# Conditioning units loaded into the accumulator a group ahead, in the first MLP of a two-layer diffusion backbone

## The chip, the cores and the metric

The kernel runs on one core of a Trainium2 chip. It uses five engines: TensorE (PE in the profile, its weight loads PEld), VectorE (DVE), ScalarE (ACT), GpSimd (POOL) and SyncE (SP), which here only issues DMA transfers from one queue. The metric is the device time of one execution in microseconds (us); lower is better. Everything is computed in float32. A product of two float32 matrices is made of three products in TensorE's fp32r format: each operand is split into a high part (a cast) and a low part (the rest, a subtraction), and high x high, high x low and low x high are summed.

## The reference

Two layers over 512 latent tokens and 256 context tokens of 1024 channels. The change lies in the first layer's MLP and in the conditioning computed beside it:

```python
def ada_mods(cond, w, b):
    m = (jax.nn.silu(cond) @ w + b)[..., None, :]
    return jnp.split(m, N_MOD, axis=-1)          # shift, scale, gate, twice

def sq_relu_mlp(h, w_in, w_out):
    return jnp.square(jax.nn.relu(h @ w_in)) @ w_out

# layer 0: mixer, then for latents and for the context, each with its own conditioning vector
x = x + gt2 * rms_norm(sq_relu_mlp(modulate(rms_norm(x, g), sh2, sc2), w_in, w_out), g_post)
```

`w_in` is 1024 x 4096, `w_out` 4096 x 1024, and `w_ada` 1024 x 6144 for each of two layers. A modulation is a vector (two of them, one for the latents and one for the context) times `w_ada`: little arithmetic, but 48 MB of weights to read.

## The kernel before, in words

The first MLP of layer 0 (`mlp0`, line 1127) has two phases. In the first, the 4096 hidden channels are made in 16 groups of 256 for all 768 tokens. Groups 2 to 15 use a Strassen-like scheme: seven products of half-size blocks instead of eight (`Seven`, line 894), each a chain of 12 matmuls of 384 columns, 84 in a group. The right-hand blocks are sums of activations made once (`sums`, tiles `sums` and `rb`), the left-hand ones sums of a group's weights (`weights_sums`, line 858), which VectorE and ScalarE make for group g + 1 while TensorE works on group g. In the profile these are the matmuls `psin<-...`. A group's results are evicted into the accumulator tile `acc` (128 partitions x 6144 floats) or, in the last group, into two tiles of the pool `work`, are squared there and leave for the DRAM tile `hidden`. Before the accumulator is needed for the second phase only its first half (3072 columns, four blocks of 768 in turn) is in use.

The second phase multiplies the hidden blocks by `w_out` in three rounds of seven products (`prep` prepares the operands of one, line 1190; matmuls `pso<-...`, 36 of 512 columns for a product), and then four plain groups. `prep(1)` makes the difference `t3` of two row blocks of `w_out` in the first 2048 columns of the accumulator; `prep(2)` and `prep(3)` use the same blocks and `t3` again. The first two hidden blocks go to the second half of the accumulator (`hid_load`), three row blocks to raw tiles (`row_load`).

Beside the first phase runs the conditioning that is due later, of three kinds of load, all of 1 MB:

- a group's weights, `sums_load(g + 2)`, issued in group g, used by `weights_sums` in the next group's turn (`raw<-in_w_mlp_in`);
- a conditioning unit, `ada_load`, half of a 1024 x 512 piece of `w_ada` for both conditioning vectors, multiplied on TensorE by `ada_mm` (4 matmuls `psada<-raw,cond`) in turn 3 of the groups 3 to 10: eight units, called 0 to 7 here;
- a lone slab, `lone_load`, 1024 x 256 of `w_ada` for the latents' vector alone, which VectorE multiplies and folds (`ada_sum`: one scaling, seven multiply-adds of 128 x 256, a transpose, a reduction into `parts`). Twelve slabs in groups 2 to 13; four make a modulation, which `ada_fin` completes with 4 selection matmuls (`psada<-parts,sel`).

All three take their tile from the ring `rawp` (line 79), three tiles of 128 x 2048, in the order in which the scheduler places them. A load waits on SyncE until the tile's last reader is done, and everything behind it on SyncE's queue waits too, because a queue issues in order. The order of every engine's instructions around the change is chosen at build time by a scheduler with its own model of times (`TC_OPTS`, line 40); the order in the program text is its input and sets which buffer a load gets. Before the change, the hidden blocks' load stands at group 15 in the text, and the scheduler has moved it up to group 2, since its place in the accumulator is free.

`raw_load` gives all 1 MB loads the same source line (L154), and nearly all engine instructions are recorded by one helper (L68), so tiles and shapes tell them apart in the profile.

Of the kernel before, what the change touches and what calls it, by code (L numbers as in the profile page):

```python
# [13 lines left out]
ALU = mybir.AluOpType  # L14
# [3 lines left out]
P = 128  # L18
D = 1024
# [34 lines left out]
def backbone(ctx: ExitStack, tc, x, c, ctx_in, c_ctx, w_ada, b_ada, g_mix_pre, g_mix_post,  # L54
# [104 lines left out]
    def work_tile():  # L159
        return tmp.tile([P, D], F32, tag="t", name="work")  # L160
# [130 lines left out]

    def ada_load(i, m, c0, width, u):
        nk = 2048 // width
        loaded[i, m, c0, u] = raw_load(w_ada[i, u * nk * P:(u + 1) * nk * P, m * D + c0:m * D + c0 + width]
                                       .rearrange("(k p) n -> p k n", p=P), width,
                                       rawp if (m, c0) == (SH2, 0) else None).rearrange("p (k n) -> p k n", n=width)
# [597 lines left out]
    class Seven:  # L894
# [11 lines left out]
        def run(self, between=None, turns={}):  # L906
# [4 lines left out]
            else:  # L911
                px, py = (psA.tile([P, 2, 512], F32, tag="a", name="psin") for _ in range(2))
                a, b, c, e = px[:, 0, 0:HN], px[:, 1, 0:HN], py[:, 0, 0:HN], py[:, 1, 0:HN]
            if g == NG - 1:
                r0, r1 = (work_tile()[:, 0:TOK] for _ in range(2))
            else:
                r0, r1 = (acc[:, TOK * z:TOK * z + TOK] for z in (2 * (g % 2), 2 * (g % 2) + 1))
            if g == 3:
# [208 lines left out]
    def mlp0(inner, order, extra, mid, last, before_last):  # L1127
# [62 lines left out]
        def prep(n):  # L1190
# [3 lines left out]
            end = c_ == NC - 1  # L1194
            t0 = X["t"] if "t" in X else acc[:, 0:2048]
            if z == 0:
                x, w = a(0, 0), b(0, 0)
            elif z == 1:
                x = done[c_, "s3"] = op(a(0, 0), a(0, 0), a(1, 0), ALU.subtract)
                w = done[c_, "t3"] = op(t0, b(1, 1), b(0, 1), ALU.subtract)  # L1200
            elif z == 2:
                x = op(X[1], a(1, 0), a(1, 1), ALU.add)
                w = op(b(0, 1), b(0, 1), b(0, 0), ALU.subtract)
            elif z == 3:
                x = op(X[0], a(1, 1), done[c_, "s3"], ALU.subtract)
                w = op(t0, done[c_, "t3"], b(0, 0), ALU.add)
            elif z == 4:
# [8 lines left out]
            wr = W[n % 3]  # L1216
            put(wr[:, 0:2048], wr[:, 2048:4096], w)
            xs[n] = [[q[:, k] for k in range(4)] for q in (hi, lo)]
# [11 lines left out]
            elif z == 6:  # L1230
                pair_load(4 * NC + 2, X[2]) if end else hid_load((c_ + 1, 1, 1), X[2])
                rows_load(4 * NC + 2) if end else row_load((c_ + 1, 1, 1))

        xs, ws = {}, {}
        for g in range(2, NG):
            now = products
            if g < NG - 1:
                products = weights_sums(g + 1)
            else:
                hid_load((0, 0, 0), acc[:, 3072:4608])  # L1240
                hid_load((0, 1, 0), acc[:, 4608:6144])
                for key in ((0, 0, 0), (0, 0, 1), (0, 1, 1)):
                    row_load(key)
            extra(g)
            seven = Seven(now, g)
            turns = {}
            if g == 2:
                turns[3] = lambda z: ada_end(*halves[1], z)
            elif g <= 10:
                half, u = halves[2 + (g - 3) // 2], (g - 3) % 2  # L1250
                ada_load(*half, 512, u)
                turns[3] = lambda z: ada_mm(*half, 512, u, z)
                if u:
                    turns[5] = lambda z: (ada_rows(*half), ada_end(*half, z))
            if g - 2 < 4 * len(lone):
                lone_load(g - 2)
            if g + 2 < NG:
                sums_load(g + 2)
            seven.run(lambda: mid(g), turns)
# [264 lines left out]
    def mid0(g):  # L1524
        n, j = divmod(g - 2, 4)
        if 0 <= n < len(lone):
            at = 32 * n + 8 * j
            ada_sum(*lone[n], j, 1, parts[0][:, at:at + 8], lone_raw.pop(g - 2))

# [5 lines left out]
    def extra0(g):  # L1535
# [4 lines left out]
        if g in (7, 8):  # L1540
            gate_away(0, GT2, g - 7)
        n, j = divmod(g - 6, 4)
        if j == 0 and 0 <= n < len(lone):
# [456 lines left out]
```

## Time and profile before

| | |
|---|---|
| Median of three runs | 1155.32 us (1154.81 to 1162.1) |
| Profiled execution | 1159.74 us, its span 1158.0 us |
| TensorE busy | 1125.4 us (97% of the span) |
| VectorE / ScalarE busy | 883.0 us (76%) / 668.7 us (58%) |
| Read from memory, written to it | 156.33 MB, 22.04 MB |
| First phase, groups 2 to 15 | about 122 to 358 us of the span |

The profile comes from one execution. A row of the timeline gives start and length in us, the engine, the operation with the tile that it writes and those it reads, shapes and a count, and in brackets the idle time before it with the work that ended it. `SPq` rows are DMA issues; a transfer lands some us later. In a row of the view of windows stand the stretch, its length, the busy time and count of each engine, and at the end the granted clock of TensorE (1.00 is full), the share of time that the DMA engines were busy, and GB/s.

### The profile page before, as it was taken

What the parts mean: (1) busy time and instruction counts of PE and PEld (TensorE: products, weight loads), DVE (VectorE), ACT (ScalarE), POOL (GpSimd) and SP (SyncE); (2) the same over time, 40 slices, a digit from 0 to 9 for tenths busy, and PEclk for the clock granted to TensorE, in tenths of its full rate; (3) what the DMA queues carried; (4) which work ended last, traced back from release to release, by engine and by line L of the source; (5) the groups of instructions that cost most, each with busy time, mean ns of one, the idle gap of its engine ahead of it and who ended that gap; (6) DMA issues with size and microseconds to landing.
All of it is one profiled execution on the core that took longest, in us unless ns stands there. A gap on an engine that the chain in (4) does not pass through costs nothing. (4 is left out here: it accounts for less than half of the span.)

```text
span 1158.0 us, 15507 instructions
## 1 busy us (share of the span) xinstructions
PE 1125.4 (97%) x6012; PEld 958.9 (83%) x6012; DVE 883.0 (76%) x1262; ACT 668.7 (58%) x1139; POOL 75.1 (6%) x82
## 2 busy tenths in 40 slices
PE   6999899999999999999999999999999999999998
PEld 5578788989988888888888889988988888888886
DVE  5799468777778887867478688977787779778875
ACT  6477345444456677765586468873775436445534
POOL 3040000000000000000231212100000000000000
PEclk9999999999999999999999999999999999999999
DMA  9996776676544443438141400046234124224304
GB/s 353 399 360 226 197 234 231 225 246 211 175 177 168 155 135 120 150 105 296 52 153 58 142 2 19 2 128 221 107 139 152 67 80 146 62 84 146 109 13 152
DMA packets 108490, 179.37 MB, mean 155 GB/s; under 512 B 7888, under 2 KB 67072, under 8 KB 108416
## 3 DMA queue, kind: packets, MB, share of 16 engines
q1 hardware_dynamic: 103712, 165.77, 42.6%
q10 hardware_dynamic: 4704, 12.61, 2.8%
q8 instruction: 47, 0.77, 0.3%
q14 instruction: 27, 0.22, 0.1%
HBM read 156.33 MB, written 22.04 MB: 154 GB/s over the span
## 5 line engine op out<-in xcount | busy, mean ns | idle before, releaser
L68 PE MATMUL pso<-rb,ra 128*128 128x512 f32 x576 | 134.9, 390 | 2.0 <-ACT m L68 1.2
L68 PEld LDWEIGHTS pso<-rb,ra 128*128 128x128 f32 x576 | 107.9, 188 | 25.5 <-ACT m L68 1.6
L68 PE MATMUL psin<-ra,rb 128*128 128x512 f32 (+2 forms) x468 | 117.5, 356 | 0.7 <-DVE acc L68 0.6
L68 DVE TENSOR_TENSOR acc<-acc,pso 128x512 f32<-128x512 f32 x90 | 60.6, 682 | 58.2 <-PE pso L68 58.2
L68 PE MATMUL psin<-ra 128*128 128x512 f32 (+1 forms) x340 | 96.3, 376 | 0.6 <-ACT work L68 0.6
L68 PEld LDWEIGHTS psin<-ra,rb 128*128 128x128 f32 x468 | 81.4, 189 | 12.7 <-issue 1.0
L68 PE MATMUL psin<-ra,units 128*128 128x384 f32 x434 | 81.8, 337 | 1.3 <-ACT psin L68 0.4
L68 PE MATMUL pso<-units,pairs 128*128 128x512 f32 x336 | 82.3, 389 | 0.0
L68 ACT CAST rb<-raw 128x2048 fp32r<-128x2048 f32 (+2 forms) x35 | 47.5, 1357 | 59.9 <-PE pso L68 54.8
L68 PEld LDWEIGHTS psin<-ra,units 128*128 128x128 f32 x434 | 75.2, 188 | 6.0 <-issue 1.7
L68 ACT CAST units<-raw 128x1024 fp32r<-128x1024 f32 (+2 forms) x47 | 49.4, 1078 | 52.9 <-DMA raw<-in_w_mlp_in 38.7
L68 PEld LDWEIGHTS pso<-units,pairs 128*128 128x128 f32 x336 | 63.1, 188 | 13.1
L68 PE MATMUL psin<-rb 128*128 128x512 f32 (+2 forms) x242 | 73.8, 357 | 0.0
L68 PEld LDWEIGHTS psin<-ra 128*128 128x128 f32 x340 | 62.7, 188 | 11.0 <-ACT work L68 1.0
L68 PE MATMUL psin<-rb,ra 128*128 128x512 f32 (+1 forms) x226 | 71.1, 367 | 0.0
L68 DVE TENSOR_TENSOR rb<-raw,rb 128x2048 fp32r<-128x2048 f32 (+2 forms) x41 | 61.3, 1494 | 10.1 <-ACT rb L68 9.9
L68 PE MATMUL psin<-sums,units 128*128 128x384 f32 x336 | 65.3, 342 | 2.7 <-ACT acc L68 2.7
L68 PEld LDWEIGHTS psin<-sums,units 128*128 128x128 f32 x336 | 59.9, 192 | 4.1 <-ACT acc L68 3.0
L68 DVE TENSOR_TENSOR units<-raw,units 128x1024 fp32r<-128x1024 f32 (+2 forms) x45 | 58.0, 1303 | 2.6 <-ACT units L68 2.5
L68 PE MATMUL pso<-units,ra 128*128 128x512 f32 x252 | 59.4, 389 | 0.0
L68 DVE TENSOR_TENSOR work<-raw 128x512 f32<-128x512 f32 (+1 forms) x42 | 35.5, 864 | 30.2 <-DMA raw<-in_w_mlp_in 25.2
L68 DVE SCALAR_TENSOR_TENSOR rows<-raw,cond,rows 128x256 f32<-128x256 f32 x112 | 53.5, 482 | 2.4
(253 smaller groups left out, 2411.0 us busy)
## 6 DMA issues: line engine op xcount, KB each, us to landing
raw<-in_w_ada SPq DMA_DIRECT2D x48, 1024.0 KB, 7.4
raw<-in_w_mlp_in SPq DMA_DIRECT2D x32, 1024.0 KB, 5.5
raw<-in_w_mlp_out SPq DMA_DIRECT2D x32, 1024.0 KB, 5.1
x<-hidden SPq DMA_DIRECT2D x14, 768.0 KB, 4.3
hidden<-acc ACTq DMA_DIRECT2D x26, 384.0 KB, 2.8
raw<-in_w_qkv SPq DMA_DIRECT2D x6, 1024.0 KB, 8.4
spill<-xl SPq DMA_DIRECT2D x8, 512.0 KB, 7.3
xl<-spill SPq DMA_DIRECT2D x8, 512.0 KB, 8.5
```

Source lines behind the costliest of these rows:

```text
L68: z = made(*args, **kw)
```

## The change

Conditioning units of groups 3 to 10 no longer take a tile of the ring. They have one home, columns 3072 to 5120 of the accumulator, and each is issued in turn 3 of the group before its own, right after the matmuls on its predecessor. In the ring remain the weights and the slabs; the weights' load is now written ahead of the slab's. A slab is folded one group after its load's group (`g - 3` instead of `g - 2`), and each `ada_fin` comes a group later. The hidden blocks' load, whose place overlaps the units' home, is written at group 14 and stands, after scheduling, behind the last unit. In the last group the results go to the accumulator as in the others; the two work tiles that they had are used by `prep(1)` for `t3`, cut in two halves with their own splits.

```diff
-    def ada_load(i, m, c0, width, u):
+    def ada_load(i, m, c0, width, u, home=None):
         nk = 2048 // width
+        if home is not None:
+            raw = loaded[i, m, c0, u] = home.rearrange("p (k n) -> p k n", n=width)
+            sy.dma_start(raw, w_ada[i, u * nk * P:(u + 1) * nk * P, m * D + c0:m * D + c0 + width]
+                         .rearrange("(k p) n -> p k n", p=P))
+            return
...
-            if g == NG - 1:
-                r0, r1 = (work_tile()[:, 0:TOK] for _ in range(2))
-            else:
-                r0, r1 = (acc[:, TOK * z:TOK * z + TOK] for z in (2 * (g % 2), 2 * (g % 2) + 1))
+            r0, r1 = (acc[:, TOK * z:TOK * z + TOK] for z in (2 * (g % 2), 2 * (g % 2) + 1))
...
-            t0 = X["t"] if "t" in X else acc[:, 0:2048]
+            t0 = X.get("t")
...
-                w = done[c_, "t3"] = op(t0, b(1, 1), b(0, 1), ALU.subtract)
+                if c_ == 0:
+                    w = done[c_, "t3"] = [op(work_tile(), b(1, 1)[:, q], b(0, 1)[:, q], ALU.subtract)
+                                          for q in (slice(0, 1024), slice(1024, 2048))]
+                else:
+                    w = done[c_, "t3"] = op(t0, b(1, 1), b(0, 1), ALU.subtract)
...
-                w = op(t0, done[c_, "t3"], b(0, 0), ALU.add)
+                if c_ == 0:
+                    for q, t3 in zip((slice(0, 1024), slice(1024, 2048)), done[c_, "t3"]):
+                        op(t0[:, q], t3, b(0, 0)[:, q], ALU.add)
+                    w = t0
+                else:
+                    w = op(t0, done[c_, "t3"], b(0, 0), ALU.add)
...
-            put(wr[:, 0:2048], wr[:, 2048:4096], w)
+            for q, src in enumerate(w if isinstance(w, list) else [w]):
+                z_ = slice(1024 * q, 1024 * q + src.shape[-1])
+                put(wr[:, 0:2048][:, z_], wr[:, 2048:4096][:, z_], src)
...
+        def unit_load(n):
+            if n < 8:
+                ada_load(*halves[2 + n // 2], 512, n % 2, acc[:, 3072:5120])
...
-            else:
+            if g == NG - 2:
                 hid_load((0, 0, 0), acc[:, 3072:4608])
                 hid_load((0, 1, 0), acc[:, 4608:6144])
+            if g == NG - 1:
                 for key in ((0, 0, 0), (0, 0, 1), (0, 1, 1)):
                     row_load(key)
...
+            if g + 2 < NG:
+                sums_load(g + 2)
+            if g - 2 < 4 * len(lone):
+                lone_load(g - 2)
             if g == 2:
-                turns[3] = lambda z: ada_end(*halves[1], z)
+                turns[3] = lambda z: (ada_end(*halves[1], z), unit_load(0))
             elif g <= 10:
                 half, u = halves[2 + (g - 3) // 2], (g - 3) % 2
-                ada_load(*half, 512, u)
-                turns[3] = lambda z: ada_mm(*half, 512, u, z)
+                turns[3] = lambda z: (ada_mm(*half, 512, u, z), unit_load(g - 2))
                 if u:
                     turns[5] = lambda z: (ada_rows(*half), ada_end(*half, z))
-            if g - 2 < 4 * len(lone):
-                lone_load(g - 2)
-            if g + 2 < NG:
-                sums_load(g + 2)
...
-        n, j = divmod(g - 2, 4)
+        n, j = divmod(g - 3, 4)
...
-            ada_sum(*lone[n], j, 1, parts[0][:, at:at + 8], lone_raw.pop(g - 2))
+            ada_sum(*lone[n], j, 1, parts[0][:, at:at + 8], lone_raw.pop(g - 3))
...
-        n, j = divmod(g - 6, 4)
+        n, j = divmod(g - 7, 4)
```

What the scheduler makes of it is read at three places. First SyncE's queue in groups 2 to 4: `raw<-in_w_mlp_in` is a group's weights, `128x8x256` of `in_w_ada` a slab, `128x4x512` of it a unit, `grows<-gc` two gate columns on their way to DRAM. Before:

```order
L154 DMA raw<-in_w_ada 128x8x256
L154 DMA raw<-in_w_mlp_in 128x8x256
L1167 DMA acc<-hidden 128x4x384 x2
L154 DMA raw<-in_w_ada 128x4x512
L411 DMA grows<-gc 128x8x1 x2
L154 DMA raw<-in_w_ada 128x8x256
L154 DMA raw<-in_w_mlp_in 128x8x256
L154 DMA raw<-in_w_ada 128x4x512
```

The same place in the changed program:

```order
L154 DMA raw<-in_w_mlp_in 128x8x256
L154 DMA raw<-in_w_ada 128x8x256
L296 DMA acc<-in_w_ada 128x4x512
L154 DMA raw<-in_w_mlp_in 128x8x256
L416 DMA grows<-gc 128x8x1 x2
L154 DMA raw<-in_w_ada 128x8x256
L296 DMA acc<-in_w_ada 128x4x512
L154 DMA raw<-in_w_mlp_in 128x8x256
```

Weights come first, the unit goes to the accumulator ahead of the next weights and of the gate columns, and the hidden blocks have left this place.

Second, VectorE from the last additions of group 14 (`acc<-acc,psin` x2) on to the split of the second product's weights in the second phase (`rb<-acc,rb` before, `rb<-work,rb` in two halves now); `rows` and `parts` belong to a slab, `x_` and `t_` are operands of the second phase. Before:

```order
L68 TENSOR_TENSOR acc<-acc,psin 128x384 x2
L68 TENSOR_TENSOR ra<-acc,ra 128x4x384
L68 TENSOR_TENSOR acc<-raw 128x2048
L68 TENSOR_TENSOR work<-work,psin 128x384
L68 TENSOR_TENSOR raw<-raw 128x2048
L68 TENSOR_TENSOR t_3133<-acc,raw 128x2048
L68 TENSOR_TENSOR work<-work,psin 128x384
L68 TENSOR_TENSOR x_3131<-acc,x_3132 128x1536
L68 TENSOR_TENSOR x_3130<-x_3132,acc 128x1536
L68 TENSOR_TENSOR rb<-acc,rb 128x2048
```

In the changed program, from the last multiply-add of the last slab:

```order
L68 SCALAR_TENSOR_TENSOR rows<-raw,cond,rows 128x256
L68 STREAM_TRANSPOSE raw<-rows 128x256
L68 TENSOR_REDUCE parts<-raw 128x8
L68 TENSOR_TENSOR acc<-acc,psin 128x384 x2
L68 TENSOR_TENSOR mods_103<-psada,cols 128x8
L68 TENSOR_TENSOR work<-raw 128x1024 x2
L68 TENSOR_TENSOR t_3128<-work,raw 128x1024
L68 TENSOR_TENSOR rb<-work,rb 128x1024
L68 TENSOR_TENSOR raw<-raw 128x2048
L68 TENSOR_TENSOR t_3128<-work,raw 128x1024
L68 TENSOR_TENSOR x_3126<-acc,x_3127 128x1536
L68 TENSOR_TENSOR x_3125<-x_3127,acc 128x1536
```

The difference of row blocks, before ahead of the last group's additions, now stands behind them and behind the last slab and its modulation; the split's second half (`rb<-work,rb`) follows the last row shown. Between the additions of group 14 and the first row shown stand the rest of that slab and the split `ra<-acc,ra`.

Third, TensorE from the last chains of group 15 (`psin`) to the second product of the second phase, with buffer numbers: `pso_3140`, `3141`, `3149` are the three tiles of the first product before, `pso_3135`, `3136`, `3144` now. Before (ten matmuls of the first tile stand further up, ahead of the last chains of group 14):

```order
L68 MATMUL psin_3015<-rb_111,ra_110 128x384 x12
L68 MATMUL pso_3140<-units_844,ra_110 128x512 x2
L68 MATMUL pso_3141<-units_844,ra_110 128x512 x12
L68 MATMUL psin_3013<-ra_110 128x384 x12
L68 MATMUL pso_3149<-units_844,ra_110 128x512 x12
L68 MATMUL pso_3163<-rb_111,ra_110 128x512
L68 MATMUL pso_3177<-rb_111,ra_110 128x512
L68 MATMUL pso_3201<-rb_111,ra_110 128x512
L68 MATMUL pso_3215<-rb_111,ra_110 128x512
L68 MATMUL pso_3163<-rb_111,ra_110 128x512 x11
```

In the changed program:

```order
L68 MATMUL psin_3007<-rb_111,ra_110 128x384 x12
L68 MATMUL pso_3135<-units_844,ra_110 128x512 x7
L68 MATMUL psada_2998<-parts_1067,sel_101 32x8 x4
L68 MATMUL psin_3005<-ra_110 128x384 x12
L68 MATMUL pso_3135<-units_844,ra_110 128x512 x5
L68 MATMUL pso_3136<-units_844,ra_110 128x512 x12
L68 MATMUL pso_3144<-units_844,ra_110 128x512 x12
L68 MATMUL pso_3158<-rb_111,ra_110 128x512
L68 MATMUL pso_3172<-rb_111,ra_110 128x512
L68 MATMUL pso_3158<-rb_111,ra_110 128x512 x6
L68 MATMUL pso_3172<-rb_111,ra_110 128x512 x6
L68 MATMUL pso_3197<-rb_111,ra_110 128x512 x7
```

All 36 matmuls of the first product now stand behind the group's next-to-last chain, with the last selection among them, and the second product starts with the matmuls that need only the first half of its weights. One matmul of the third product (`pso_3211`) follows, and then the rest of `pso_3158`, which needs the second half.

## The prediction

> **What bounds the kernel now.** I read the head of the page first, then who made TensorE wait in the stretch that the change touches (126 to 365 us), then the timeline around each of those waits.
>
> ```profile
> span 1158.0 us, 15507 instructions
> PE 1125.4 (97%) x6012; PEld 958.9 (83%) x6012; DVE 883.0 (76%) x1262; ACT 668.7 (58%) x1139; POOL 75.1 (6%) x82
> PE psin L68 <- ACT acc L68: 3.7, 3, 2.7
> PE psada L68 <- DMA raw<-in_w_ada: 3.4, 1, 3.4
> PE psada L68 <- DVE parts L68: 2.0, 1, 2.0
> PE pso L68 <- ACT m L68: 1.2, 1, 1.2
> PE psin L68 <- DVE acc L68: 0.6, 1, 0.6
> PE pso L68 <- DVE rb L68: 0.5, 1, 0.5
> ```
>
> TensorE bounds the program: 97% of the span. No matmul is removed, so the change can win only what TensorE loses in this stretch. The waits (columns: total us, times, longest) come to 11.4 us in the six rows. What a wait does to the clock is added to them:
>
> ```profile
> 140.20:143.50 3.30, 2.91 (x7) 1.25 (x8) 0.00 (x0) 0.00 (x0) 0.00 (x0) 0.50 0.66 39
> 191.40:194.70 3.30, 3.30 (x12) 3.30 (x11) 3.30 (x7) 1.52 (x3) 0.00 (x0) 0.50 0.32 117
> 331.70:336.00 4.30, 4.30 (x32) 4.28 (x33) 3.61 (x3) 2.62 (x3) 0.00 (x0) 1.00 1.04 409
> 166.22 4.32 PE L68 MATMUL psin<-ra,units 128*128 128x384 f32 x24
> 190.67 6.00 PE L68 MATMUL psin<-sums,units 128*128 128x384 f32 x24 [2.73 <-ACT acc L68]
> ```
>
> The third figure from the end of a window row is the granted clock. It was 0.50 right after the two longest waits and stayed 1.00 after the 2.0 us wait. The last two rows give its price: the same 24 matmuls took 4.32 us at full clock and 6.00 us after the wait, so 1.68 us. I put the same 1.7 us on the other long wait. The 4.32 us also give the pace: (4.32 - 0.34) / 23 = 0.173 us for a matmul of 384 columns; a group of 84 such matmuls is some 14.5 us, about 15.5 with its conditioning matmuls.
>
> The Trainium skill, "TensorE: Matmul & The Clock Gate", Part 1, says that the clock halves after an idle window of about 3.4 us or more. By that rule the wait of 2.73 us would have cost no clock, and the gain below would be 1.7 us smaller. The trace does not agree: 2.73 us was enough here, and the measurement decides.
>
> **Part 1, units in the accumulator, a group ahead.** The first long wait is for a conditioning unit:
>
> ```profile
> 126.36 0.92 SPq L1167 DMA_DIRECT2D acc<-hidden  x2
> 127.61 0.37 SPq L154 DMA_DIRECT2D raw<-in_w_ada  x1
> 132.97 2.35 PE L68 MATMUL psin<-rb 128*128 128x384 f32 x12
> 140.59 1.92 PE L68 MATMUL psada<-raw,cond 128*32 128x512 f32 x4 [3.35 <-DMA raw<-in_w_ada]
> DMA to landing us min/median/max: 5.0/6.6/12.9
> ```
>
> Unit 0 was issued at 127.61, behind 1.5 MB of hidden blocks (126.36), and TensorE idled 3.35 us for it. The last row is for the weight, slab and unit loads (1 MB each) issued from 115 to 345 us. In the changed queue the unit stands third after the loads that were issued at 116 and 117 us, and the hidden blocks have gone to the end of the phase. Three loads in a row at the shortest time land at 117.3 + 3 x 5.0 = 132.3. TensorE asks two matmuls after the row at 132.97 is through, at about 135.5. So this wait goes with its clock loss: 3.35 + 1.7 = **5.05 us**. What covers the load is 3 us of margin; each further us of lateness costs one.
>
> The write of two gate columns with 4-byte pieces stays on the queue, now behind unit 0 and the next weights. The slab and the unit after it wait there for that write's data, but both have a group of time.
>
> The seven later units have one home. A load can start only when the matmuls on the unit before it are through. In the changed order 74 to 144 matmuls of 384 columns stand between uses (12.8 us and more), but for one pair, units 1 and 2: there only 38 stand between, 38 x 0.173 = 6.6 us and some 0.1 for the tiny ones. Nearest rows: 5.0 us at the shortest, 6.6 the median, 12.9 at most. So the wait is 0 to 6.2 us, with 1.7 for the clock from 2.7 on. I take 0: the load of 12.9 us had hidden blocks and 4-byte writes around it, and here the weight load stands behind the unit.
>
> **Part 2, weights first in a ring of three that is theirs and the slabs'.**
>
> ```profile
> 178.84 1.06 PE L68 MATMUL psada<-raw,cond 128*32 128x512 f32 x8
> 179.97 0.37 SPq L154 DMA_DIRECT2D raw<-in_w_mlp_in  x1
> 188.46 1.05 ACT L68 CAST units<-raw 128x1024 fp32r<-128x1024 f32 x1 [3.73 <-DMA raw<-in_w_mlp_in]
> 190.16 0.46 ACT L68 COPY acc<-psin 128x384 f32<-128x384 f32 x1
> ACT units L68 <- DMA raw<-in_w_mlp_in: 38.7, 10, 6.8
> ```
>
> This is the second long wait, read backwards. TensorE idled to 190.67 for an eviction by ScalarE (190.16). That engine had stood in its order behind the cast of group 7's weights until they landed at 188.46. They were issued at 179.97, right after TensorE finished the conditioning matmuls of 178.84: the weights had to take that unit's slot. With the units elsewhere, a weight load takes the slot of the slab or the weights of a group earlier, freed about 15 us before. It then lands near 175 to 178 us, 10 us ahead of its cast. So 2.73 + 1.68 = **4.41 us** go. The row of 38.7 us (ten times that ScalarE waited for weights) shrinks too, but TensorE stands in none of the others, so I count nothing for them.
>
> SyncE's queue is in order, so the price of the new arrangement is that each weight load stands behind a slab that waits for the weights before it to be used, and behind a unit that waits for TensorE. All three come free early in a group, and the weights are asked for a group later, so this is hidden by 15 us less one landing, 5.0 to 12.9 us.
>
> **Part 3, slabs a group later.**
>
> ```profile
> 326.03 3.60 DVE L68 SCALAR_TENSOR_TENSOR rows<-raw,cond,rows 128x256 f32<-128x256 f32 x7
> 329.67 0.45 DVE L68 STREAM_TRANSPOSE raw<-rows 128x256 f32<-128x256 f32 x1
> 331.14 0.41 DVE L68 TENSOR_REDUCE parts<-raw 128x8 f32<-128x256 f32 x1
> 331.61 0.25 PE L68 MATMUL psada<-parts,sel 128*32 128x8 f32 x8 [2.01 <-DVE parts L68]
> ```
>
> The selection matmuls of the last slabs stood too early in TensorE's order and idled it for **2.01 us**, with no clock loss. In the changed order the folding of the last slab stands on VectorE ahead of the last group's two additions, and the selection behind the matmuls of the product that the second addition reads. Nothing waits there. The slab's work on VectorE (the 3.60 us and the short steps quoted) moves by a group and adds nothing.
>
> **Part 4, the step to the second matmul.** Here a wait changes its cause.
>
> ```profile
> 344.00 1.76 DVE L68 TENSOR_TENSOR ra<-acc,ra 128x1536 fp32r<-128x1536 f32 x1 [2.62 <-ACT ra L68]
> 350.87 2.24 PE L68 MATMUL psin<-rb,ra 128*128 128x384 f32 x12
> 350.88 2.29 DVE L68 TENSOR_TENSOR acc<-raw 128x2048 f32<-128x2048 f32 x1 [5.12 <-DMA hidden<-acc]
> 358.43 1.75 DVE L68 TENSOR_TENSOR x<-acc,x 128x1536 f32<-128x1536 f32 x1
> 361.77 2.28 DVE L68 TENSOR_TENSOR rb<-acc,rb 128x2048 fp32r<-128x2048 f32 x1
> 364.10 11.20 PE L68 MATMUL pso<-rb,ra 128*128 128x512 f32 x48 [0.55 <-DVE rb L68]
> DMA to landing us min/median/max: 5.0/5.0/8.3
> L68 DVE TENSOR_TENSOR units<-raw,units 128x1024 fp32r<-128x1024 f32 x12 | 14.6, 1220 | 0.0
> ```
>
> Before, the first difference of weight blocks (350.88) waited for the accumulator to be written out, its split ended at 361.77 + 2.28, and TensorE lost 1.2 + 0.5 us. Call T the end of the product at 350.87, so 353.1 there. In the changed program that difference goes to two work tiles, but stands on VectorE behind the last slab, the last additions and the sum of the selection, and needs the third block of rows, whose slot the last slab holds. The split at 344.00 ended at T - 7.3; ten matmuls of the second phase (2.3 us) no longer stand between, so T - 5.0; the slab's last multiply-add, transpose and reduction behind it (3.60 / 7 + 0.45 + 0.41 = 1.4) make T - 3.6 for the issue. It lands 5.0 to 8.3 us later (the row of landings, for the loads of 320 to 372 us): T + 1.4 to T + 4.7. The selection, seven matmuls of the second phase after T, allows T + 2 at the earliest. So the difference starts at S = T + 2 to T + 4.7; I take T + 2.5, since 5.0 is the median landing too.
>
> From S, VectorE has, in this order, two half differences, a half sum, a half split, a whole difference, a half sum, two x operations and the other half split: six halves of 1.22 (the mean in the last row), 2.28 and 2 x 1.75, in all 13.1 us. Cutting one operation in two costs 2 x 1.22 - 2.28 = 0.16 us, three times; it is in this sum. TensorE has 36 matmuls of 512 columns (11.20 / 48 = 0.23 us each), 12 of 384 and 22 more of 512 before it needs the other half: 8.3 + 2.1 + 5.1 = 15.5 us after T. S + 13.1 = T + 15.6, so hardly a wait. Three VectorE operations further (2.28 + 2.28 + 1.75 = 6.3) against 22 matmuls (5.1) it is T + 21.9 against T + 20.6, about 1.3 us. Between the ends the wait is 0.8 to 3.5 us, and 1.7 for the clock at the top. Against 1.7 us before I take **0**, with -0.9 to +3.5 as bounds. That the last group's results lie in the accumulator costs nothing: the same evictions write another place, free since group 13's results went out.
>
> **Sum.** 5.05 + 4.41 + 2.01 + 0 = 11.5 us off the profiled execution's 1159.74 us: 1148.3. (The span is 1158.0; 1.7 us lie around it and stay.) That execution is 4.4 us above the median shown (1155.32, of 1154.81 to 1162.1), which is just what one of the two long waits costs. If the usual run lacks one of them, the median comes down by 7.1 to 1148.2; if the 4.4 us are of another kind, by 11.5 to 1143.8. The first has the better reason, since the waits are races between transfers; I lean a little to the other side: **1147 us**.
>
> **The rivals.**
>
> *One home is too few.* Unit 2 lands late after unit 1, in the 38 matmuls. For it: 6.6 us is the median landing and also all the time there is. Against: the unit is first in its queue then. At 9 us the wait is 2.4 us, at 12.9 us 6.2 + 1.7: 1149 to 1155. Chance 0.13. The Trainium skill ("Trainium Kernel Development and Optimization", Best Practices) asks for double buffers to overlap transfers with work, and by it this home speaks against the change; the trace of before cannot show it.
>
> *The weights stay late.* The queue is in order, so a slab that waits holds the weights behind it, and the second long wait returns somewhere: 4.4 us less gain, 1151. For it: 38.7 us of such waits now. Against: the slack of a whole group. Chance 0.12.
>
> *Slower: the step to the second matmul.* The last slab holds the third row block's slot. If that block lands 8.3 us after a slab that itself was folded a group's half late (7 us), S is T + 12, the waits there are 12 + 13.1 + 6.3 - 20.6 = 10.8 us and two clock losses, 14.2 us in all, against 1.7 before: it eats the 11.5 us. From S = T + 12 on it is slower: 1156 to 1168. Against: slabs landed well before use in the rows above. Chance 0.05, most of it under 1%.
>
> *More goes than I count.* The small waits (1.0 of the row of 3.7 beside its 2.7, the row of 0.6) and the step's 1.7 go too and the 4.4 us are not a wait: 1143 or below. Chance 0.2.
>
> *It does not do what it says.* The scheduler could place the unit loads late; the order shows them a group ahead. Chance 0.02.
>
> **How the numbers follow.** My case has 0.48. About 1% (11.6 us) is what a measurement of this kernel can tell from no change, so it divides at 1143.8 and 1166.9. Faster by over 1% is the case of more, 0.2; slower by over 1% is the far part of the slower rival and of unforeseen waits in a new order, 0.03; the rest, 0.77, lies within. The range runs from 1142 (most of the case of more) to 1154 (both late-load rivals); what is left out is the slow step and the far end of the gain.
>
> **What would show it.** In the changed profile: no clock of 0.50 near 140 or 191 us; units landing before their matmuls, with unit 2 the nearest; ScalarE's wait for weights well under 38.7 us; no wait for the slabs' sums; and at the step a wait of 0 to 3 us for VectorE. Wrong would be a TensorE wait of over 2.7 us on a unit, on weights, or on the first split of the second phase.

## The result and the profile after

| us | before | after |
|---|---|---|
| median, measured side by side | 1158.12 | 1142.01 |
| spread of the times | 1154.81 to 1162.1 | 1141.47 to 1142.33 |
| ratio of the times, 95% interval | | 0.9859, 0.982 to 0.9898 |
| profiled execution | 1159.74 | 1141.98 |
| its span | 1158.0 | 1140.2 |

The change is faster by 1.4%: 16.1 us by the medians and 17.8 us by the two profiled executions. The median before is higher than the 1155.32 us given ahead of the prediction because a fourth time, 1160.91 us, has come to those three. The forecast was 1147 us, with most of the chance on a change of less than 1%; the gain is larger than that, and the time lies on the lower edge of the range of 1142 to 1154 us. In all the runs below one execution was slow (1269.16 us at a granted clock of 0.831, in the kernel "the same order without the home"); it counts in that kernel's median and not in its ratio.

TensorE's line in the head of the page after:

```profile
PE 1118.7 (98%) x6012; PEld 957.0 (84%) x6012; DVE 882.4 (77%) x1265; ACT 669.9 (59%) x1140; POOL 75.1 (7%) x82
```

The same 6012 matmuls are busy 6.7 us less (1125.4 before), and TensorE is idle 11.1 us less (span less busy time: 32.6 before, 21.5 now). The first figure is more than the two half-clock periods cost; what else is in it comes out below. Who makes TensorE wait from 115 to 370 us, after (columns as before: total us, times, longest):

```profile
PE pso L68 <- DVE ra L68: 0.3, 1, 0.3
PE psin L68 <- DVE mods L68: 0.3, 1, 0.3
```

Before, the six longest rows had 11.4 us there; now 0.6 us are left, and the granted clock is 1.00 throughout that stretch. The waits that I had counted went, and so did those that I had not. The timeline of after at the place of the old second wait (SyncE's queue, TensorE, ScalarE):

```profile
166.34 0.37 SPq L296 DMA_DIRECT2D acc<-in_w_ada  x1
171.28 0.37 SPq L154 DMA_DIRECT2D raw<-in_w_mlp_in  x1
...
173.58 1.06 PE L68 MATMUL psada<-acc,cond 128*32 128x512 f32 x8
...
176.56 1.05 ACT L68 CAST units<-raw 128x1024 fp32r<-128x1024 f32 x1 [0.84 <-DMA raw<-in_w_mlp_in]
```

The page's row of the units' loads after (count, size, median us to landing), and then ScalarE's waits for weights from 126 to 345 us:

```profile
acc<-in_w_ada SPq DMA_DIRECT2D x8, 1024.0 KB, 5.3
```

```profile
ACT units L68 <- DMA raw<-in_w_mlp_in: 9.6, 5, 5.2
```

Group 7's weights are issued 8.7 us earlier than before (171.28 against 179.97) and cast at 176.56 against 188.46. Unit 2, the one that I feared for, is issued at 166.34 and lands after 5.1 us, some 2 us before its matmuls (173.58). The slowest unit load is that of unit 1: issued at 140.12 behind the two writes of gate columns, it takes 19.0 us to land, still 6 us before its matmuls at 165.21. ScalarE's waits for weights fell from 38.7 to 9.6 us. The timeline of after at the step to the second matmul, VectorE and then TensorE:

```profile
336.91 2.36 DVE L68 TENSOR_TENSOR work<-raw 128x1024 f32<-128x1024 f32 x2 [0.39 <-DMA raw<-in_w_mlp_out]
339.18 1.22 DVE L68 TENSOR_TENSOR t<-work,raw 128x1024 f32<-128x1024 f32 x1
...
353.67 3.42 DVE L68 TENSOR_TENSOR ra<-x,ra 128x1536 fp32r<-128x1536 f32 x2
...
332.24 2.24 PE L68 MATMUL psin<-rb,ra 128*128 128x384 f32 x12
...
355.47 2.83 PE L68 MATMUL pso<-rb,ra 128*128 128x512 f32 x11 [0.30 <-DVE ra L68]
```

In the prediction's terms T, the end of the product at 332.24, is 334.48, so the difference starts at T + 2.4 (I had T + 2.5) and waits for the third row block, as said. TensorE waits 0.30 us at T + 21.0; I had 1.3 us there.

### The profile page after: what moved, and what is told of

It reads as the page before. It is cut to its first block, busy times and chain, and to the rows that moved or that the text cites. A ratio compares the mean times of both kernels' runs of the same rounds, so it can differ in the third digit from the quotient of the medians.

```text
span 1140.2 us, 15534 instructions
## 1 busy us (share of the span) xinstructions
PE 1118.7 (98%) x6012; PEld 957.0 (84%) x6012; DVE 882.4 (77%) x1265; ACT 669.9 (59%) x1140; POOL 75.1 (7%) x82
## 5 line engine op out<-in xcount | busy, mean ns | idle before, releaser
L68 PEld LDWEIGHTS psin<-ra 128*128 128x128 f32 x340 | 62.6, 188 | 10.9 <-ACT work L68 1.0
L68 PEld LDWEIGHTS pso<-units,ra 128*128 128x128 f32 x252 | 47.3, 188 | 9.7
```

What stands on the lines that cost most here:

```text
L68: z = made(*args, **kw)
```

## The experiments

All times are compared with the kernel before on the same chip in the same comparison; its median was 1157.58 us for the first four runs, 1158.34 for the next four, 1159.06 for the last three. "The stretch" is the time from the first `psin<-sums` matmul to the 250th of `pso`, the same 1529 matmuls in every kernel: 289.4 us before, 271.2 after. Two questions stood: which of the parts brings the gain, and why it is larger than the sum. The letters of the theories are those of each expectation.

### One part alone, or one part undone

**The kernel before once more**, to see which of its waits come again.

> The kernel before, unchanged, once more with a profile. Its times lie in two groups, 1154.8 and 1155.3 against 1159.7 to 1162.1 us. If the two groups differ by one of the two long waits with its half clock (2.73 + 1.68 + 0.28 = 4.7 us, or 5.3 us for the other), a profile of about 1155 us shows one stretch of half clock in 126 to 365 us where the profile of 1159.7 us has two; if it shows both, the difference lies elsewhere. A profile of about 1160 us shows the same waits as the first and tells nothing new.

Measured: 1157.83 us, ratio 1.0003 (0.9978 to 1.0028), single times from 1155.17 to 1163.28. TensorE's two longest waits in the execution profiled there:

```profile
PE psin L68 <- ACT units L68: 6.0, 1, 6.0
PE pso L68 <- ACT m L68: 1.2, 1, 1.2
```

It took 1157.18 us, near the first profile's 1159.74, by other waits: the 3.4 us for unit 0 are gone and 6.0 us for group 5's weights have come. So a list of waits from one execution is one draw; what the two have in common is that loads come late.

**The home alone.** The kernel before with `home=`, `unit_load` and the load a group ahead; weights still behind the slab, slabs and second phase as before.

```
...
-                ada_load(*half, 512, u)
-                turns[3] = lambda z: ada_mm(*half, 512, u, z)
+                turns[3] = lambda z: (ada_mm(*half, 512, u, z), unit_load(g - 2))
```

> The kernel before with the units' home in the accumulator and their load a group ahead, and nothing else: slabs first, weights second, slabs folded at once, old step to the second matmul. Theory A (the units' place in the ring caused both long waits, and a wait costs TensorE its shown idle time, 0.28 us more for draining and refilling, and 1.7 us of half clock from about 2.7 us on): the two long waits go, 3.35 + 1.7 + 2.73 + 1.68 + 0.56 = 10.0 us; the wait for the slabs' sums (2.0) and the step's (1.7) may stay: 1146 to 1150 us against about 1158 before and 1142.0 after. Theory B (the order weights before slabs did it): the wait behind late weights stays, with its half clock, so 4.7 us less is gained: 1151 to 1154 us.

Measured: 1157.22 us, ratio 1.0011 (0.9995 to 1.0027). No gain can be seen, and both theories, which expected 1146 to 1150 and 1151 to 1154, fall. TensorE's longest wait:

```profile
PE psin L68 <- ACT acc L68: 6.8, 1, 6.8
```

SyncE's queue in the timeline of the same kernel:

```profile
131.08 0.37 SPq L154 DMA_DIRECT2D raw<-in_w_ada  x1
136.56 0.99 SPq L416 DMA_DIRECT2D grows<-gc  x2
137.89 0.37 SPq L154 DMA_DIRECT2D raw<-in_w_mlp_in  x1
```

And the group view of the last of these loads: who waited for it, and its landing:

```profile
  ACT units L68: 10.6, 1
...
DMA to landing us min/median/max: 15.9/15.9/15.9
```

The wait for a tile is gone and the weights of group 5 are late all the same: they stand behind the two writes of gate columns, whose issue waits for VectorE until 136.56, and then take 15.9 us to land. ScalarE waits 10.6 us for them and TensorE 6.8 us for ScalarE.

**The step as it was.** The changed kernel with the last group's results in work tiles and the whole difference `t3` in the accumulator.

```
...
-                    w = done[c_, "t3"] = [op(work_tile(), ...) for q in (...)]
...
+                w = done[c_, "t3"] = op(t0, b(1, 1), b(0, 1), ALU.subtract)
...
```

> The changed kernel with the old step to the second matmul: the last group's results in two work tiles, the difference t3 whole and in the accumulator. Theory A: the step's waits of before come back and nothing else, 1.19 + 0.55 + 2 x 0.28 = 2.3 us, less the 0.3 + 0.28 us that the new step has: 1143.7 us, at most 1144.5. Theory C (the step was worth nothing, as the prediction had it): 1142.0 within 0.5 us.

Measured: 1146.35 us, ratio 0.9916 (0.9888 to 0.9944): 4.3 us above the changed kernel, and above what either theory expected. In its profile the cost is one wait of 3.2 us with 6.8 us of half clock from 347.9 on; its row:

```profile
PE pso L68 <- ACT ra L68: 3.2, 1, 3.2
```

That is more than the 1.2 + 0.5 us which the same step cost before. The new order of the loads is not the reason: the kernel "home, and weights before the slab" below has that order and the old step too, and waits 1.2 + 0.5 us as before. What sets it apart is that it folds the slabs a group earlier (the hidden blocks' load is written at another place, but issued at the same one, 258.31 against 258.04). Three rows show what the later slabs do here. First come the difference on VectorE and the load of the third row block in this kernel, then the same difference in the kernel with the slabs folded at once:

```profile
336.62 2.29 DVE L68 TENSOR_TENSOR acc<-raw 128x2048 f32<-128x2048 f32 x1 [0.51 <-DMA raw<-in_w_mlp_out]
331.46 0.37 SPq L154 DMA_DIRECT2D raw<-in_w_mlp_out  x1
```

```profile
334.72 2.29 DVE L68 TENSOR_TENSOR acc<-raw 128x2048 f32<-128x2048 f32 x1 [5.12 <-DMA hidden<-acc]
```

The last slab holds the third row block's tile. VectorE is through with that slab at 331.44, the block is issued at 331.46, and the difference waits for it; with the slabs folded at once the block is issued near 312, and the difference waits only for the accumulator to be written out. The halves make up for the lateness that the later slabs bring, and for the old wait besides.

**The unit in its own group.** The changed kernel with the unit's load written in the group that uses it, still into the home.

```
-                turns[3] = lambda z: (ada_mm(*half, 512, u, z), unit_load(g - 2))
+                unit_load(g - 3)
+                turns[3] = lambda z: ada_mm(*half, 512, u, z)
```

> The changed kernel with each unit's load written in its own group, behind that group's weights and slab, but still into the home in the accumulator: a home of its own without the group ahead. Theory A (what matters is that units leave the ring): the weights stay early, so no half clock after a wait for weights; the first unit, written in group 3, may be late again: 3.35 + 1.7 + 0.28 = 5.3 us at most, 1142 to 1147.5 us. Theory D (loading a group ahead is what gains): several units are late, each 1 to 3 us and more with half clock: 1148 to 1156 us.

Measured: 1142.1 us, ratio 0.9875 (0.9847 to 0.9904), and two waits of 0.4 and 0.3 us. That the load is written a group ahead is worth nothing: the scheduler issues the first units within 0.5 us of the times that they have in the changed kernel (165.90 against 166.34 for unit 2). What it needs is the home.

### The order of the loads

**Home, and weights before the slab.** As "the home alone", with two calls exchanged.

```
-            if g - 2 < 4 * len(lone):
-                lone_load(g - 2)
             if g + 2 < NG:
                 sums_load(g + 2)
+            if g - 2 < 4 * len(lone):
+                lone_load(g - 2)
```

> The kernel before, with the units' home and the load a group ahead, and a group's weights issued before its slab; slabs folded and selected as before, second phase as before. Theory A (what made the weights late was their place behind the slab and behind the two writes of gate columns, whose issue waits for VectorE; the home alone cannot show its gain): group 5's weights are issued near 131 us, no TensorE wait of over 2.5 us is left in groups 2 to 14, and what stays over the changed kernel's 1142.0 is the slabs' wait (2.0 us and 0.3 for the restart) and the old step (some 1.4 to 4.3): 1145 to 1149 us. Theory B (the order of weights and slab is worth little, the later slabs did it): as with the home alone, 1156 to 1158.

Measured: 1144.21 us, ratio 0.9878 (0.9855 to 0.99): 14.1 of the 16 us. Its longest waits:

```profile
PE pso L68 <- ACT m L68: 1.2, 1, 1.2
PE pso L68 <- DVE rb L68: 0.5, 1, 0.5
```

This is theory A, 0.8 us better than the range that it gave, because the wait for the slabs' sums is gone though the slabs are folded as before. Most of what is left is the old step, which also brings one period of half clock.

**The same order without the home.** The kernel before with the weights and then the slab ahead of the unit in each group; units in the ring of three tiles.

```
+            if g + 2 < NG:
+                sums_load(g + 2)
+            if g - 2 < 4 * len(lone):
+                lone_load(g - 2)
             if g == 2:
...
-            if g - 2 < 4 * len(lone):
-                lone_load(g - 2)
-            if g + 2 < NG:
-                sums_load(g + 2)
```

> The kernel before with one thing changed: in each group the loads of weights and slab, weights first, stand ahead of the unit's load. Units keep sharing the three raw tiles, without a home. Theory A (the home is needed to free the slot): a load still has to wait for TensorE to be through with a unit, so at least one wait of 3 to 6 us with its clock loss stays, for a unit or for weights: 1150 to 1158. Theory D (the order alone is the gain, the home is not needed): 1145 to 1149.

Measured: 1151.04 us, ratio 0.9933 (0.9912 to 0.9954), with one long wait, for a unit whose load could be issued only at 145.46, when VectorE was through with the slab in its tile:

```profile
PE psada L68 <- DMA raw<-in_w_ada: 2.6, 1, 2.6
```

Order alone 7.3 us, home alone nothing, both 14.1 us: the two need each other. (Order and later slabs without a home was not run. By my reading three tiles do not hold all three kinds of load then; no run shows it.)

**Slabs at once.** The changed kernel with the slabs folded and selected where they were before.

```
-        n, j = divmod(g - 3, 4)
+        n, j = divmod(g - 2, 4)
...
```

> The changed kernel with one part undone: a lone slab is folded in the group after its load and its sums selected there, as before. Theory A (a wait costs its idle time and some 0.3 us for emptying and refilling TensorE): the wait of 2.0 us for the slabs' sums returns, 1144.3 us, or up to 1146 if it falls wholly into one window of the clock. Theory B (with the weights in time VectorE is early enough anyway): 1142.0. Theory E (the slab that is folded earlier also frees its tile earlier, and the weights gain): no more than 1142, with waits shorter than 0.5 us.

Measured: 1141.41 us, ratio 0.9851 (0.9826 to 0.9876), no wait over 0.4 us. This fits theory B, and theory E as well; theory A falls. Part 3 of the change gains nothing, and with the old step it did harm, as the step as it was shows. So the halves are worth less than the 4.3 us found there: with the slabs folded at once they take the kernel from 1144.21 us (home, weights first) to 1141.41, 2.8 us. VectorE was late for the slabs because it had stood waiting for weights. The row

```profile
DVE work L68 <- DMA raw<-in_w_mlp_in: 25.2, 11, 4.8
```

is its row in the kernel before (126 to 345 us), and in the changed kernel it is

```profile
DVE work L68 <- DMA raw<-in_w_mlp_in: 6.9, 6, 2.2
```

**The slab before the weights.** The changed kernel with those two calls alone exchanged back.

> The changed kernel with one part undone: in each group the slab's load stands ahead of the weights' load again, so group 5's weights stand behind the writes of gate columns. Theory C: they are issued near 138 us and land near 153, TensorE waits 5 to 7 us there and loses up to 3.4 us of clock: 1150 to 1154. Theory B (the later slabs free their tiles early enough, the order of the two loads is worth little): 1142 to 1144.

Measured: 1160.47 us, ratio 1.0017 (1.0001 to 1.0033). That is far worse than the 1150 to 1154 expected: one exchanged pair of calls takes back the whole change.

TensorE's waits:

```profile
PE psin L68 <- ACT acc L68: 6.9, 1, 6.9
PE psin L68 <- DVE units L68: 1.9, 2, 1.3
PE pso L68 <- DVE rb L68: 1.0, 2, 0.6
```

ScalarE's from 126 to 345 us:

```profile
ACT units L68 <- DMA raw<-in_w_mlp_in: 33.1, 9, 10.7
```

The first of TensorE's rows is the wait that the home alone had, here with 10.2 us of half clock. ScalarE's row, and TensorE's smaller ones, show that the weights are late in later groups too.

### The writes of gate columns

**At groups 11 and 12.** The home alone, with the two writes moved out of the units' stretch (VectorE's products for them are kept in the written order).

```
-        if g in (7, 8):
-            gate_away(0, GT2, g - 7)
+        if g in (11, 12):
+            gate_away(0, GT2, g - 11)
```

> The home alone once more (weights behind the slab as before), but the two gate columns are made and written at groups 11 and 12, out of the units' stretch. Theory C (the writes of gate columns hold the weights up: their issue waits for VectorE until 136.6 us, and the weights stand behind): group 5's weights are issued near 132 us and land near 140, in time; the wait of 6.8 us and its clock loss of 3.4 go: 1146 to 1149. Theory A in its narrow form (it is the slab that must not stand in front): the weights land after the slab, still too late, 1152 to 1157.

Measured: 1162.5 us, ratio 1.0045 (1.0026 to 1.0063): a miss for both theories by time, and the clearest run by profile. TensorE waits nowhere from 125 to 275 us. Then it waits 2.9 and 10.9 us:

```profile
PE psin L68 <- ACT acc L68: 11.6, 2, 10.9
PE psin L68 <- ACT units L68: 2.9, 1, 2.9
```

Both are for weights that now stand behind a write, in the timeline of its queue:

```profile
263.08 0.36 SPq L416 DMA_DIRECT2D grows<-gc  x1
263.73 0.37 SPq L154 DMA_DIRECT2D raw<-in_w_mlp_in  x1
...
286.65 0.53 SPq L416 DMA_DIRECT2D grows<-gc  x1
287.32 1.47 SPq L154 DMA_DIRECT2D raw<-in_w_mlp_in  x1
```

The load of 263.73 landed after 13.9 us. The trouble moved with the writes.

**Behind everything.** The home alone, with both writes placed in group 14, behind the last weights, slabs and row blocks of the phase; and **the same without the home**.

```
...
     def mid0(g):
+        if g == 14:
+            gate_away(0, GT2, 0)
+            gate_away(0, GT2, 1)
...
-        if g in (7, 8):
-            gate_away(0, GT2, g - 7)
```

> The home alone (weights behind the slab, slabs and step as before), with the two writes of gate columns put behind the last weights, slabs and row blocks of the phase. Theory C (a load that stands behind such a write lands some 15 us after its issue instead of 5 to 6; that is what made the weights late, and their place behind the slab costs little by itself): no TensorE wait over 1.5 us in groups 2 to 15, and the time of the kernel with the home and the weights first, 1144 to 1147. Theory A in its narrow form (weights behind the slab are late for themselves): some of the waits return, 1149 to 1156.

> The kernel before with only the two writes of gate columns moved, behind the last weights, slabs and row blocks of the phase. Theory C (they are the whole cause): 1144 to 1148. Theory A (the tile that a unit holds and the hidden blocks ahead of unit 0 are causes of their own): the wait for unit 0 (up to 3.4 us and 1.7 for the clock) and the one for a tile (2.7 and 1.7) stay in part: 1149 to 1155. Theory B (the writes do not matter here): 1156 to 1160.

Measured: with the home 1153.78 us, ratio 0.996 (0.9943 to 0.9977); without it 1157.85, ratio 0.9994 (0.9976 to 1.0012). The profiled executions, 1157.35 and 1163.41 us, were each the longest of their kernel. With the home TensorE does not wait at all from 125 to 300 us, with the weights behind the slab in every group. So theory C is right on that stretch, and wrong on the time, because waits come at the end:

```profile
PE pso L68 <- ACT m L68: 3.3, 1, 3.3
PE psada L68 <- DVE parts L68: 2.3, 1, 2.3
PE psin L68 <- DVE work L68: 2.1, 1, 2.1
```

The timeline of the kernel with the home there, SyncE's queue and VectorE:

```profile
331.81 0.99 SPq L416 DMA_DIRECT2D grows<-gc  x2
...
345.97 2.29 DVE L68 TENSOR_TENSOR acc<-raw 128x2048 f32<-128x2048 f32 x1 [9.89 <-DMA hidden<-acc]
```

The old step waits for the accumulator to be written out, by a transfer of ScalarE's queue. With the gate columns' writes on their way from 331.81, that transfer, issued at 338.62, took 7.1 us to land, against 2.3 us for the one issued at 348.30 in the kernel before; VectorE waits 9.89 us instead of 5.12. The wait for the slabs' sums, 2.3 us, is there too: from 290 to 335 us VectorE waits 8.9 us for weights, which still stand behind a slab, against 2.3 us where they stand ahead of it. Without the home the old wait behind a unit's tile returns (3.0 us near 186 us, for group 7's weights), as theory A said. By its time that kernel lies in the range of theory B, for which the writes do not matter; but the new waits at the end hide what it gained by their move, so its time decides nothing. Not run is the changed kernel with these writes at the end, so how much they still cost there, with the weights ahead of them, stays open.

### What a wait costs

From the profile of each kernel I took TensorE's idle time in the stretch, 0.28 us more for every wait, and half of the half-clock time in which it worked. 270.6 us is what is left of the changed kernel's stretch without these, so the first row comes out by construction.

| kernel | idle | waits | clock loss | 270.6 + sum | stretch |
|---|---|---|---|---|---|
| after | 0.30 | 1 | 0 | 271.2 | 271.2 |
| home, weights first | 2.10 | 3 | 1.71 | 275.2 | 274.8 |
| the step as it was | 3.17 | 1 | 3.03 | 277.1 | 276.8 |
| weights first, no home | 7.01 | 8 | 1.64 | 281.5 | 280.4 |
| home, gates last | 8.96 | 5 | 4.79 | 285.7 | 285.2 |
| home alone | 11.06 | 5 | 3.38 | 286.4 | 286.6 |
| before, again | 9.53 | 5 | 4.64 | 286.2 | 287.2 |
| slab before weights | 12.03 | 9 | 3.05 | 288.2 | 290.3 |
| before | 12.06 | 11 | 3.21 | 288.9 | 289.4 |
| home, gates later | 16.43 | 6 | 3.51 | 292.2 | 291.8 |
| gates last, no home | 12.58 | 10 | 6.54 | 292.5 | 292.9 |

Of the other ten rows nine come out within 1.1 us. In the slab-first kernel 2.1 us are left over, and I do not know what they are. The 0.28 us is read from waits that stand alone, such as this one of before:

```profile
305.11 0.86 PE L68 MATMUL psin<-ra,units 128*128 128x384 f32 x4
306.62 0.45 PE L68 MATMUL psin<-sums,rb 128*128 128x384 f32 x1 [0.66 <-ACT acc L68]
306.91 0.34 PE L68 MATMUL psin<-rb 128*128 128x384 f32 x1
```

A matmul lasts 0.34 us, but the next one starts 0.173 us after it. Before the wait the overlap is lost: the last of the four began at 305.97 - 0.34 = 305.63, its successor was due at 305.80 and came at 306.62, 0.82 us late though only 0.66 idle. After it the second matmul starts 0.29 us later, not 0.17. Together 0.16 + 0.12 = 0.28 us. Both parts count as busy time: the ten waits fewer at 0.28 us and the clock loss of 3.2 make 6.0 of the 6.7 us by which TensorE's busy time fell.

## Why the prediction was wrong

The mechanism was right in outline: late loads made TensorE wait, and these waits went. The sum was too small, the base that it was taken from was chosen wrongly, and the gain was given to the wrong parts of the change.

- **The step that failed: "5.05 + 4.41 + 2.01 + 0 = 11.5".** By the table's method the stretch before loses 12.06 + 11 x 0.28 + 3.21 = 18.35 us. I counted 3.35 + 2.73 + 2.01 of idle time and 3.38 of clock. Left out were 2.2 us of small waits, 1.7 us at the step, and 3.1 us for emptying and refilling TensorE eleven times. The changed kernel keeps 0.6. So 17.8 us were there to be won, and the two profiled executions differ by 17.8. (The stretches differ by some 18.2; the rest is lost again outside.)
- **The small waits** I put into a rival ("more goes than I count", 0.2). They had the same cause as the long ones: engines behind schedule because of late weights (38.7 us of ScalarE's waits, 25.2 of VectorE's). I saw the row of 38.7 us and counted nothing for it, because TensorE stood in none of these waits directly. That rival came true, but partly by luck: it started from 1155.32, some 3 us too low, and knew nothing of the 3.1 us of refilling, which made up for it.
- **The base.** I took the 4.4 us between the profiled execution and the median of 1155.32 for one of the two long waits, absent in the usual run. The repeat shows that executions of before lose about the same by different waits. Three times were a small sample of a spread of 1151.8 to 1163.2 us, whose median later was 1157.6 to 1159.1. The profiled execution was not 4.4 but 1.6 us above the median (1158.12), and none of that was a wait missing elsewhere. Taken from 1158.12, the sum of 11.5 gives 1146.6, so my 1147 agrees with it by luck; the error of the time is that of the sum.
- **Part 1, 5.05 us.** Unit 0 comes in time, as said. But the home alone gains nothing, so this part has no price of its own: without the new order the wait moves on to the next late load.
- **Part 2, 4.41 us.** The wait for group 7's weights was read rightly as the unit's tile: it goes with the home, and without the home it stays when the writes are moved. But it is only half of why weights are late. The other half is the writes of gate columns ahead of group 5's weights, which cost 6.8 us with the home alone. I named these writes on the changed queue, as harmless there, and did not see on the old queue that they were a cause.
- **Part 3, 2.01 us.** This wait went, but not through the later slabs: with the weights first the slabs come in time wherever they are folded. I said that the later folding adds nothing; with the old step it made the wait there larger (3.2 us against 1.2 + 0.5).
- **Part 4, 0 with -0.9 to +3.5.** The step gained 1.44 us of idle time, which is beyond the lower bound. S was right (T + 2.4 for T + 2.5); the wait was 0.30 instead of 1.3 us, since VectorE starts an operation some 0.1 us before the one ahead of it is recorded as ended, which adds up eleven times from 336.91 to the first half of the row at 353.67. With the step as it was, the changed kernel is 4.3 us slower; with the slabs folded at once the halves are worth 2.8 us.
- **One home is too few** did not come true: unit 2 had about 2 us to spare. The Trainium skill, "Trainium Kernel Development and Optimization", Best Practices, asks for double buffers; here one was enough, as the profile after shows no TensorE wait on a unit. No run has two homes.
- **The weights stay late** and **slower at the step** did not come true either. But the first is what the kernel with the slab in front shows at its full price: 1160.5, not the 1151 that I gave it.

## What to carry to other kernels

When several engines wait for the same late loads, the rows of TensorE's waits in one execution are a sample: price the cause by all of them, small ones too, and give each wait its idle time, its refill and its share of a half-clock window. In an in-order queue look for what stands directly ahead of an urgent load; a tiny transfer in small pieces there can cost more than a megabyte. Two edits that each remove one of two causes of the same lateness show their full gain only together (here 0 and 7.3 us alone, 14.1 together), so test them one at a time and together. And undo each part of a change that won: here the later slabs and the load a group ahead could be undone, each by itself, at no cost.

## What the runs showed of the hardware

**The half clock comes by windows.** The half-clock periods of one execution all begin on one grid of 3.413 us and last one, two or three steps of it, but for the one with which every profile ends. What decides in these profiles is the idle time inside one step, not the length of a wait. TensorE's busy time in a step and the clock in the next, before and then the home alone (columns: us; busy us and instructions of PE, PEld, DVE, ACT and POOL; the granted clock; transfer share, GB/s):

```profile
327.91:331.32 3.41, 1.68 (x10) 1.36 (x8) 3.27 (x7) 3.39 (x7) 0.00 (x0) 1.00 0.95 281
331.32:334.73 3.41, 3.12 (x25) 3.10 (x26) 2.57 (x4) 1.73 (x3) 0.00 (x0) 1.00 1.04 410
```

```profile
325.88:329.29 3.41, 1.60 (x16) 1.58 (x17) 2.60 (x5) 2.67 (x4) 0.00 (x0) 1.00 0.92 333
329.29:332.70 3.41, 3.41 (x13) 3.41 (x12) 2.83 (x2) 1.77 (x2) 0.00 (x0) 0.50 1.04 402
```

1.73 us idle kept the clock, 1.81 us halved it. Over all 13 profiles, the end of the program left out, steps at full clock with 1.74 us idle or more (16 of them) were all followed by half clock, those with 1.64 or less by none, and of two with 1.73 one was: about half a step. So the two waits of the step, 1.2 + 0.5 us, cost no clock in one profile of before and 1.7 us in the other. The Trainium skill, "TensorE: Matmul & The Clock Gate", Part 1, has the free-running window of 3413 ns, and the grid agrees; but it asks for a whole idle window, and here half of one was enough. The same page, Part 2, "Single matmul latency", puts the fixed part of a lone bf16 matmul's time at some 166 ns at full clock, and says that a stream hides the drain; the 0.16 us lost ahead of the wait at 306.62 is of that size, with other operands.

**Transfers of 4-byte pieces slow what comes behind them.** The weights of group 5 were issued at 137.89 us behind two such writes of 4 KB each, and at 137.15 without them. All transfers from 136 to 150 us, the home alone (with the writes) and then with the writes last:

```profile
DMA packets 2733, 0.68 MB, mean 48 GB/s; under 512 B 2081, under 2 KB 2733, under 8 KB 2733
raw<-in_w_mlp_in SPq DMA_DIRECT2D x1, 1024.0 KB, 15.9
```

```profile
DMA packets 1857, 2.90 MB, mean 207 GB/s; under 512 B 64, under 2 KB 1088, under 8 KB 1856
raw<-in_w_mlp_in SPq DMA_DIRECT2D x1, 1024.0 KB, 5.3
```

Issued within a microsecond of the same time, the load landed after 15.9 us in the one and after 5.3 in the other. 8 KB of writes delayed the load behind them by some 10 us. Transfers of the other queue were slow beside them too: the accumulator's write-out took 7.1 us instead of 2.3, as shown above. What inside the transfer engines does it, the profiles do not show.
